# Attention chunk 7 scored and normalized between the last two blocks of the key/value projection

## The chip, the cores and the metric

The kernel runs on one core of one Trainium2 chip, as one launch. Its time is the device time of a whole execution in microseconds (us), median of several. The core's engines run side by side, each with a queue of its own that it works off in order: TensorE (PE, with its weight loads PEld), VectorE (DVE), ScalarE (ACT), GpSimd (POOL) and SyncE (SP), which here issues the transfers (DMA). An instruction that waits holds up all that stands behind it in its engine's queue.

## The reference

One step of a two-layer encoder: layer 0 is an mLSTM mixer with an MLP, layer 1 attention over a band of chunks with an MLP. A prompt of 1024 rows (16 chunks of 64) and a sample of 32 rows with 512 cached rows of keys and values are computed in float32. Layer 1's attention, cut:

```python
kv = (x * (1 + kv_scale) + kv_shift) @ p['w_kv']          # 4 key heads and 4 value heads of 64
q = (u @ p['w_q_b'][lb]).reshape(Bsz, S, NH_B, HD_B)      # 16 query heads, 4 to each key head
def one_chunk(args):                                      # one chunk of 64 queries
    ci, qb = args
    kb = lax.dynamic_slice_in_dim(kp, ci * CHUNK, span, axis=1)   # its own chunk and the 8 before: 576 keys
    vb = lax.dynamic_slice_in_dim(vp, ci * CHUNK, span, axis=1)
    s = jnp.einsum('bqkgd,bskd->bkgqs', qb, kb) * (HD_B ** -0.5) + bias
    s = jnp.where(valid, s, -jnp.inf)
    p = jax.nn.softmax(s, axis=-1)
    return jnp.einsum('bkgqs,bskd->bqkgd', p, vb)
y = o @ p['w_out_b'][lb]
```

A chunk c below 8 has fewer valid keys: (c + 1) * 64, so chunk 7 has 512, and chunks 8 to 15 have 576.

## The kernel before, in words

A matmul operand in float32 is held as two parts, a rounded one (`hi`) and the rest (`lo`); keys are two arrays, `k0` and `k1` (`kk`). SBUF is shared out by tagged rings: `raw` has 3 buffers (inputs and weights as loaded), `wc` 6, the temporary tiles 5. A tile that takes a buffer waits until the last reader of the buffer's former tile is done, and so does a transfer into it.

**The key/value loop** goes over 9 blocks t of rows (8 of 128 prompt rows, one of the 32 sample rows). Block t's input `uk_t` was loaded and split two blocks earlier (`kv_input`); 24 matmuls make the keys, 24 the values (`kv0_t`, `kv1_t`). ACT copies the values to `V`. `put_keys` splits the keys (`kd0` on ACT, `kd1` on DVE), PE transposes them (`kt_n<t>`, and `kt_c<t>` for the cached keys), and four casts on ACT fill `k0` and four on DVE `k1`. The helper `flow` runs pieces of `put_keys` between later blocks' matmuls, so the keys of block 7 are cast after the last block, 8.

**Attention** is a list `todo` of groups (gp, c, e): pair of key heads gp, chunk c (16 is the sample), e one of the pair. A group has two units (query pairs; the sample one). `softmax_unit` makes scores `s` on PE, adds the bias and takes the row extreme in one DVE reduction, and exponentiates on ACT into a tile `p`. `normalize` has a reciprocal on DVE and scales `p` on POOL. `transposed` turns `p` on PE (`pt`), and ACT and DVE copy it in turn to `pT`. `weighted_values` multiplies with `V` (`pv`) and splits the result into `QO`. Names carry the group: `s_0_8_01` is gp 0, chunk 8, e 0, unit 1. PE's queue is in the order in which the program is written: in step n of the loop group n is scored, group n-1 normalized, group n-3 transposed and the pair that ended with n-4 multiplied with `V`. The instructions of the other engines are ordered by the framework's scheduler, which places each by an estimate of when its operands are there, the loads and casts of weights included.

A counter `nun` numbers the units, and its value modulo 12 sets the buffer of `p`: 0 to 4 a temporary tile, 5 to 7 a `raw` tile, 8 to 11 a tile of the attention's own pool. The first blocks of the output weights, `w_ob0_0` and `w_ob0_1` (`wo_block`, `wtile`), are loaded during attention, each in a `raw` buffer (`raw_ob0_0`, `raw_ob0_1`); ACT (L89) and DVE (L90) split them as they split any weight. The issue is written in the list behind the groups (1, 15, e=1) and (1, 9, e=1). Of the output projection (`op_b`), `w_ob0_0` and `w_ob0_1` are the first weights, and `w_ob1_0` the next. The bias table comes in four tiles, `bias0` to `bias3`, loaded after the last block into `wc` buffers.

Of the kernel before, what the change touches and what calls it, by code (L numbers as in the profile page):

```python
# [8 lines left out]
F32 = mybir.dt.float32  # L9
# [6 lines left out]
P = 128  # L16
D = 1024
KC = D // P
TP = 1024
# [56 lines left out]
def trunk_kernel(ctx: ExitStack, tc: tile.TileContext, a, o):  # L76
# [7 lines left out]
    def raw_tile(shape, name):  # L84
        return ring.tile(shape, F32, tag="raw", name=name, bufs=3)
# [99 lines left out]
    def bank(name):  # L185

        bank_n[0] += 1
        return (tpt, nmt, adat, mmt, tpt, nmt, mmt, mmt)[bank_n[0] % 8](name)
# [661 lines left out]
    def tmp_t(shape, name, dt=F32):  # L850
        return T_.tile(shape, dt, tag="t", name=name, bufs=5)
# [847 lines left out]
    def put_keys(src, m, pos, nm):  # L1699

        kd = [tmp_t([P, 256], f"kd{i}_{nm}", F32R) for i in range(2)]
        nc.scalar.copy(kd[0][:m], src)
        nc.vector.tensor_sub(kd[1][:m], src, kd[0][:m].bitcast(F32))
        yield
        ps = bank(f"kt_{nm}").rearrange("p (i b t) -> p i b t", i=2, b=2)
        for i in range(2):
            for b in range(2):
                nc.tensor.transpose(ps[:, i, b, :m], kd[i][:m, b * P:(b + 1) * P].bitcast(F32), ident[:m, :m])
        for i in range(2):
            for g0 in range(2):  # L1710
                for half in range(2):
                    dst = kk[i][64 * half:64 * half + 64, g0::2, pos:pos + m]
                    KCOPY[i][half != g0](dst, ps[64 * g0:64 * g0 + 64, i, :, :m])
# [10 lines left out]
    def kv_input(t):  # L1724
        m = P if t < NT - 1 else TS
        cnd = 0 if t < NT - 1 else 1
        xr = raw_tile([P, KC, P], f"x1_{t}")
        nc.sync.dma_start(xr[:, :, :m], xsp[1][:, :, t * P:t * P + m])
        uk = ring.tile([P, 2, KC, P], F32R, tag="wc", name=f"uk_{t}", bufs=6)
        if m < P:  # L1730
            nc.vector.memset(uk.bitcast(F32), 0.0)
        x = xr[:, :, :m]
        nc.gpsimd.tensor_mul(x, x, kvsc[:, :, cnd:cnd + 1].broadcast_to([P, KC, m]))
        nc.vector.tensor_add(x, x, kvsh[:, :, cnd:cnd + 1].broadcast_to([P, KC, m]))
        split(uk[:, 0, :, :m], uk[:, 1, :, :m], x)
        return uk
# [3 lines left out]
    def cached_keys(t):  # L1740
        cr = tmp_t([P, 256], f"ck_{t}")
        nc.sync.dma_start(cr, ck[t * P:(t + 1) * P])
        nc.sync.dma_start(V[:, 8 + t], cv[t * P:(t + 1) * P])
        yield 3.0
        yield from put_keys(cr, P, TP + t * P, f"c{t}")
    for t in range(NT):
        if t % 2 == 0 and t < 8:
            flow.add(cached_keys(t // 2))
        m = P if t < NT - 1 else TS
        uk = uks[t]  # L1750
        pk = [bank(f"kv{i}_{t}")[:, :256] for i in range(2)]
        for i in range(2):
            for k in range(KC):
                w = wkv[i][k // 4]
                nc.tensor.matmul(pk[i], uk[:, 0, k], w[:, 0, k % 4], start=(k == 0), stop=False)
                nc.tensor.matmul(pk[i], uk[:, 0, k], w[:, 1, k % 4], start=False, stop=False)
                nc.tensor.matmul(pk[i], uk[:, 1, k], w[:, 0, k % 4], start=False, stop=(k == KC - 1))
            if i == 0:
                flow.tick()
        vi = t if t < NT - 1 else 12  # L1760
        nc.scalar.copy(V[:m, vi], pk[1][:m])
        flow.add(put_keys(pk[0][:m], m, t * P if t < NT - 1 else TP + 512, f"n{t}"))
        flow.tick()
        if t >= 4:
            ks = tmp_t([P, 256], f"ks_{t}")
            nc.scalar.copy(ks[:m], pk[0][:m])
            dk, dv = (o["k_p"], o["v_p"]) if t < NT - 1 else (o["k_s"], o["v_s"])
            r0 = (t - 4) * P if t < NT - 1 else 0
            nc.sync.dma_start(dk[0, r0:r0 + m].rearrange("s g d -> s (g d)"), ks[:m])
            nc.sync.dma_start(dv[0, r0:r0 + m].rearrange("s g d -> s (g d)"), V[:m, vi])  # L1770
        if t + 2 < NT:
            uks.append(kv_input(t + 2))
    flow.finish()
    ps0.__exit__(None, None, None)


    at_cm = tc.tile_pool(name="attn", bufs=1, reuse_waits="tile")
    at = at_cm.__enter__()
    psT_cm = tc.tile_pool(name="psT", bufs=1, space=PSUM, reuse_waits="tile")
    psT = psT_cm.__enter__()  # L1780
    bias, sbias = [], []
    for i, (nb, ns) in enumerate(((3, 0), (3, 0), (2, 1), (0, 3))):
        bt = ring.tile([P, 2112], F32, tag="wc", name=f"bias{i}", bufs=6)
        b3 = bt[:, :nb * 576].rearrange("p (b j) -> p b j", j=576) if nb else None
        for hd in range(2 if nb else 0):
            h0 = 2 * len(bias) + hd
            nc.sync.dma_start(b3[64 * hd:64 * hd + 64], bias_d[h0:h0 + 2 * nb - 1:2].rearrange("h i j -> i h j"))
        s3 = bt[:, nb * 576:nb * 576 + ns * 544].rearrange("p (b j) -> p b j", j=544) if ns else None
        for r in range(4 if ns else 0):
            h0 = 4 * len(sbias) + r  # L1790
            nc.sync.dma_start(s3[32 * r:32 * r + 32],
                              bias_d[h0:h0 + 4 * ns - 3:4, :32, :544].rearrange("h i j -> i h j"))
        bias += [b3[:, j] for j in range(nb)]
        sbias += [s3[:, j] for j in range(ns)]

    nun = [0]

    def softmax_unit(qst, g, k0, nk, bt, off, mx, nm):


        s = psT.tile([P, 2, 512], F32, tag="s", name=f"s_{nm}", bufs=2)
        parts = [(0, 0, nk)] if nk <= 512 else [(0, 0, nk // 2), (1, nk // 2, nk // 2)]
        for b, j0, w in parts:
            for i in range(2):
                nc.tensor.matmul(s[:, b, :w], qst, kk[i][:, g, k0 + j0:k0 + j0 + w], start=(i == 0), stop=(i == 1))  # L1805
        nun[0] += 1
        i = nun[0] % 12
        p = tmp_t([P, 640], f"p_{nm}") if i < 5 else raw_tile([P, 640], f"p_{nm}") if i < 8 else \
            at.tile([P, 640], F32, tag="p", name=f"p_{nm}", bufs=4)
        if off:  # L1810
            nc.gpsimd.memset(p[:, :off], 0.0)
        z = p[:, off:off + nk]
        w = parts[0][2]
        np_ = len(parts)
        nc.vector.tensor_tensor_reduce(out=z.rearrange("p (b w) -> p b w", b=np_), in0=s[:, :np_, :w],  # L1815
                                       in1=bt.rearrange("p (b w) -> p b w", b=np_), op0=ALU.add, op1=ALU.min,
                                       scale=-0.125, scalar=3e38, accum_out=mx[:, 0:1])
        nc.scalar.activation(z, z, AF.Exp, bias=mx[:, 0:1], scale=-1.0, accum_out=mx[:, 1:2])
        return p, z
# [50 lines left out]
    class Group:  # L1870
# [15 lines left out]
        def scores(self, pr):  # L1886
            if pr >= self.n:
                return
            bt = bias[2 * self.g + pr][:, 576 - self.nk:] if self.c < 16 else sbias[self.g]
            self.units.append(softmax_unit(qo(self.c)[:, self.e, self.gp, pr * P:(pr + 1) * P], self.g, self.k0, self.nk,  # L1890
                                           bt, self.off, self.mx[:, :, pr], f"{self.nm}_{self.e}{pr}"))

# [25 lines left out]
    for gp in range(2):  # L1918
        for i in range(17):
            c = slim[gp][i // 2] if i % 2 else wide[i // 2] if i < 16 else slim[gp][8]  # L1920
            todo += [(gp, c, e, gp and e and i in (8, 11)) for e in range(2)]
    groups = {}
    with tc.manual_schedule(engines={mybir.EngineType.PE}):
        for n in range(len(todo) + 4):
            new, old, done = n if n < len(todo) else None, groups.get(n - 3), groups.pop(n - 4, None)
            if done and done.e:
                done.values()
            if new is not None:
                groups[n] = Group(*todo[n][:3])
                groups[n].scores(0)  # L1930
            if groups.get(n - 1):
                normalize(groups[n - 1].units, groups[n - 1].mx)
            turn = old.turn() if old else iter(())
            next(turn, None)
            if new is not None:
                groups[n].scores(1)
            for _ in turn:
                pass
            if new is not None and todo[n][3]:
                wo_pre[0, len(wo_pre)] = wo_block(0, len(wo_pre))  # L1940
# [159 lines left out]
```

## Time and profile before

| what | value |
| --- | --- |
| median of 3 runs | 2428.24 us (2427.45 to 2430.74) |
| the profiled execution | 2430.01 us |
| its span in the trace | 2427.9 us |
| PE busy | 97% |
| DVE busy | 81% |
| ACT busy | 49% |
| mean granted PE clock | 0.993 |
| key/value loop ends, attention starts | about 1412 us into the span |
| attention ends, output projection starts | 1616.6 us |

The profiled execution is 1.8 us longer than the median, and 2.1 us of it lie outside the span. Times of places in the trace count from the span's start. PE's busy time includes that at a reduced clock, so a slow stretch does not show as idle: the column of the granted clock shows it.

### The profile page before, as it was taken

The page shows a single profiled execution, that of the slowest core. Times are in us where ns is not written, and L with a number is a line of the kernel's source. Part 1 is how long each engine was busy: PE and PEld are TensorE (multiplying, and loading weights), DVE is VectorE, ACT ScalarE, POOL GpSimd, SP SyncE. Part 2 cuts the span into 40 slices and gives each one's busy share as a digit, 9 for nine tenths or more (in the row PEclk, how much of TensorE's full clock was granted, in tenths as well). Part 3 has the DMA queues.
Part 4 walks back from the last instruction along what each step waited for, and adds up shares of the span by engine and source line. Part 5 has one row for each costly group of instructions (what it writes and reads, how often), then busy time and mean ns, then how long its engine had stood idle before and what let it go on. Part 6 is the DMA issues. An engine that isn't in the chain of part 4 may idle for free.

```text
span 2427.9 us, 44306 instructions
## 1 busy us (share of the span) xinstructions
PE 2361.4 (97%) x17180; PEld 2265.5 (93%) x17180; DVE 1973.8 (81%) x4094; ACT 1180.5 (49%) x2394; POOL 166.5 (7%) x315
## 2 busy tenths in 40 slices
PE   7999999999999999999999999999999999899997
PEld 4999999999999999999989977789999999899997
DVE  4899897778788789989887666756998888887878
ACT  4544456278566630000147466764776777222212
POOL 0111100000000000000001124420000000000003
PEclk9999999999999999999999999999999999999999
DMA  8432322436556896576413220042586779966642
GB/s 295 124 112 87 108 81 90 161 109 206 183 184 203 290 345 244 211 263 216 162 62 100 69 70 1 10 121 57 168 279 222 257 259 337 367 245 235 228 149 72
DMA packets 283702, 423.60 MB, mean 174 GB/s; under 512 B 15320, under 2 KB 205164, under 8 KB 278372
## 3 DMA queue, kind: packets, MB, share of 16 engines
q1 hardware_dynamic: 279460, 390.50, 48.3%
q10 hardware_dynamic: 4032, 30.28, 3.1%
q8 instruction: 135, 2.21, 0.4%
q14 instruction: 75, 0.61, 0.1%
HBM read 304.91 MB, written 118.17 MB: 174 GB/s over the span
## 4 chain that ended last, share of the span: by engine, by line
PE 50%; DVE 10%; DMA 4%; ACT 4%; issue 2%; POOL 1%; SPq 0%; ACTq 0%; DVEq 0%; POOLq 0%
PE dn L1424 11%; PE up L1289 8%; PE dn L120 4%; PE dn L119 4%; PE dn L118 4%; PE pv L1862 3%; PE s L1805 2%; PE pt L1840 2%; DMA radw<-in_w_ada_dram 2%; PE op_b L118 1%; PE op_b L119 1%; DVE wf_u L90 1%; PE op_b L120 1%; DMA rdn_u<-in_w_up_dram 1%; PE up L120 1%
## 5 line engine op out<-in xcount | busy, mean ns | idle before, releaser
L1054 DVE SCALAR_TENSOR_TENSOR ACX<-dn,ada,ACX 128x264 f32<-128x264 f32 (+6 forms) x664 | 281.5, 447 | 84.6 <-PE dn L1424 41.3
L1424 PE MATMUL dn<-fx,wf_d 128*128 128x264 f32 x2016 | 254.0, 285 | 6.4 <-DVE ACX L1054 4.0
L1424 PEld LDWEIGHTS dn<-fx,wf_d 128*128 128x128 f32 x2016 | 248.7, 188 | 8.7 <-DVE ACX L1054 2.7
L89 ACT CAST w_dn<-raw_dn 128x1024 fp32r<-128x1024 f32 x36 | 37.7, 1051 | 284.0 <-DMA raw_dn<-in_w_down_dram 133.1
L118 PE MATMUL dn<-hs,w_dn 128*128 128x384 f32 (+2 forms) x512 | 161.0, 315 | 0.0
L119 PE MATMUL dn<-hs,w_dn 128*128 128x384 f32 (+2 forms) x512 | 160.9, 315 | 0.0
L120 PE MATMUL dn<-hs,w_dn 128*128 128x384 f32 (+2 forms) x512 | 156.4, 314 | 1.3 <-DVE w_dn L90 1.3
L1289 PE MATMUL up<-TF,wf_u 128*128 128x264 f32 x1056 | 143.4, 285 | 3.8 <-ACT H L1292 3.8
L1289 PE MATMUL up<-U,wf_u 128*128 128x264 f32 x1056 | 140.1, 285 | 2.5 <-DVE H L1295 2.0
L1289 PE MATMUL up<-u,wf_u 128*128 128x264 f32 x1056 | 139.7, 285 | 1.6 <-ACT wf_u L89 0.6
L277 DVE SCALAR_TENSOR_TENSOR aw<-radw,cs,aw 128x512 f32<-128x512 f32 x196 | 139.3, 743 | 0.8 <-DMA radw<-in_w_ada_dram 0.8
L1289 PEld LDWEIGHTS up<-TF,wf_u 128*128 128x128 f32 x1056 | 134.2, 188 | 5.1 <-ACT H L1292 5.1
L1289 PEld LDWEIGHTS up<-U,wf_u 128*128 128x128 f32 x1056 | 133.1, 188 | 4.0 <-DVE H L1295 3.0
L1289 PEld LDWEIGHTS up<-u,wf_u 128*128 128x128 f32 x1056 | 132.6, 188 | 2.5 <-ACT wf_u L89 0.8
L119 PE MATMUL dn<-U,w_dn 128*128 128x384 f32 (+2 forms) x416 | 129.8, 313 | 0.0
L118 PE MATMUL dn<-U,w_dn 128*128 128x384 f32 (+2 forms) x416 | 129.4, 312 | 0.3 <-DVE ada L302 0.3
L120 PE MATMUL dn<-U,w_dn 128*128 128x384 f32 (+2 forms) x416 | 125.5, 312 | 0.6 <-DVE w_dn L90 0.6
L120 PEld LDWEIGHTS dn<-hs,w_dn 128*128 128x128 f32 x512 | 95.9, 188 | 2.1 <-DVE w_dn L90 1.7
L119 PEld LDWEIGHTS dn<-hs,w_dn 128*128 128x128 f32 x512 | 96.5, 188 | 0.0
L118 PEld LDWEIGHTS dn<-hs,w_dn 128*128 128x128 f32 x512 | 96.4, 188 | 0.1
L1815 DVE CUSTOM_DVE_ANT_0 p<-s,bias 128x576 f32<-128x576 f32 (+9 forms) x132 | 79.1, 605 | 20.2 <-PE s L1805 13.4
L90 DVE TENSOR_TENSOR HL<-H,HL 128x1056 fp32r<-128x1056 f32 x64 | 80.3, 1254 | 17.5 <-ACT HL L89 17.5
(394 smaller groups left out, 7167.5 us busy)
## 6 DMA issues: line engine op xcount, KB each, us to landing
hpl<-HL SPq DMA_DIRECT2D x144, 264.0 KB
rdn_u<-in_w_up_dram SPq DMA_DIRECT2D x64, 512.0 KB
hd<-HL SPq DMA_DIRECT2D x28, 1056.0 KB
fx<-hd SPq DMA_DIRECT2D x50, 528.0 KB
radw<-in_w_ada_dram SPq DMA_DIRECT2D x24, 1024.0 KB
hd<-HM SPq DMA_DIRECT2D x28, 792.0 KB
raw_up<-in_w_up_dram SPq DMA_DIRECT2D x40, 512.0 KB
raw_dn<-in_w_down_dram SPq DMA_DIRECT2D x36, 512.0 KB
```

The lines of the kernel that those rows point to most:

```text
L90: (eng or nc.vector).tensor_sub(dst_l, src, dst_h.bitcast(F32))
L118: nc.tensor.matmul(ps, wh, mov(0, k), start=(k == 0), stop=False)
L119: nc.tensor.matmul(ps, wh, mov(1, k), start=False, stop=False)
L120: nc.tensor.matmul(ps, wl, mov(0, k), start=False, stop=(k == nk - 1))
L277: nc.vector.scalar_tensor_tensor(acc[cnd], raw[:, k], sc, acc[cnd], op0=ALU.mult, op1=ALU.add)
L1054: nc.vector.scalar_tensor_tensor(xs, ps[:, off + o:off + o + mm_], gate[:, fc, cnd:cnd + 1], xs, op0=ALU.mult, op1=ALU.add)
L1289: nc.tensor.matmul(p, self.ws[w][:, wl, k], moving(f, tp, xl, k), start=first and k + n_ == 0, stop=k == 3 and n_ == 2, skip_group_check=n ...
L1424: nc.tensor.matmul(p, ws[w][:, wl, k], t[:, s0, xl], start=first and k + n_ == 0, stop=k == kg - 1 and n_ == 2, skip_group_check=not first)
L1805: nc.tensor.matmul(s[:, b, :w], qst, kk[i][:, g, k0 + j0:k0 + j0 + w], start=(i == 0), stop=(i == 1))
L1815: nc.vector.tensor_tensor_reduce(out=z.rearrange("p (b w) -> p b w", b=np_), in0=s[:, :np_, :w], in1=bt.rearrange("p (b w) -> p b w", b=np ...
L1840: nc.tensor.transpose(pt[:kp, j - j0, pr * P:(pr + 1) * P], ps_[pr][:, j * P:j * P + kp], ident)
L1862: nc.tensor.matmul(pv[64 * e:64 * e + 64, :nq], V[:kp, vt0 + j, g * 64:(g + 1) * 64], pts[e][:kp, j, :nq], start=(j == 0), stop=(j == nt - 1))
```

## The change

Chunk 7 with the first pair of key heads (groups (0, 7, 0) and (0, 7, 1)) goes to the front of the list. Its scores, reductions, exponentials, and the normalization of e = 0, are placed into the key/value loop: e = 0 ahead of block 7, e = 1 ahead of block 8. The scores take a PSUM bank of the loop's pool. The bias columns that chunk 7 needs are loaded a second time, into two `raw` tiles (`near_0`, `near_1`; 0.5 MB each). The tiles `bias0` to `bias2` are issued after blocks 6, 7 and 8, `bias3` after the loop. The counter `nun` starts at 7, so that chunk 7's four `p` tiles lie in the attention's own pool, and all later units have a number 7 higher than before (chunk 7 of the first pair comes ahead of chunk 8 now). The attention loop starts at step 2 and has the transposes of chunk 7 between the scores of chunk 8. From the scores of the third list entry onward, PE's queue is the former one. The functions `softmax_unit` to `wo_block` are only moved up in the file, ahead of the loop; of them `softmax_unit` and `scores` change in one expression. The diff, cut:

```diff
+    nun, near, groups = [7], {}, {}
-    nun = [0]
...
-        s = psT.tile([P, 2, 512], F32, tag="s", name=f"s_{nm}", bufs=2)
+        s = bank(f"s_{nm}")[:, None] if near else psT.tile([P, 2, 512], F32, tag="s", name=f"s_{nm}", bufs=2)
...
-            bt = bias[2 * self.g + pr][:, 576 - self.nk:] if self.c < 16 else sbias[self.g]
+            bt = near[self.e][:, pr] if near else \
+                bias[2 * self.g + pr][:, 576 - self.nk:] if self.c < 16 else sbias[self.g]
...
     wide, slim = (8, 12, 13, 14, 15, 9, 10, 11), ((7, 6, 5, 4, 16, 3, 2, 1, 0), (16, 7, 6, 5, 4, 3, 2, 1, 0))
             c = slim[gp][i // 2] if i % 2 else wide[i // 2] if i < 16 else slim[gp][8]
+            if not gp and i < 2:
+                c = 7 + i
...
+    def near_bias(e):
+        b = raw_tile([P, 2, 512], f"near_{e}")
+        for hd in range(2):
+            nc.sync.dma_start(b[64 * hd:64 * hd + 64],
+                              bias_d[4 * e + hd:4 * e + hd + 3:2, :, 64:576].rearrange("h i j -> i h j"))
+        return b
+
+    def early(n):
+        groups[n] = Group(*todo[n][:3])
+        for pr in range(2):
+            groups[n].scores(pr)
+        if n:
+            normalize(groups[0].units, groups[0].mx)
+
     for t in range(NT):
         if t % 2 == 0 and t < 8:
             flow.add(cached_keys(t // 2))
+        if t >= NT - 2:
+            early(t - NT + 2)
...
         if t + 2 < NT:
             uks.append(kv_input(t + 2))
+        if t == NT - 3:
+            near.update({e: near_bias(e) for e in range(2)})
+        if t >= NT - 3:
+            bias_load(t - NT + 3)
     flow.finish()
+    near.clear()
     ps0.__exit__(None, None, None)
+    bias_load(3)
...
-        for n in range(len(todo) + 4):
-            new, old, done = n if n < len(todo) else None, groups.get(n - 3), groups.pop(n - 4, None)
-            if done and done.e:
+        for n in range(2, len(todo) + 4):
+            new, done = n if n < len(todo) else None, groups.pop(n - 4, None)
+            old = groups.get(n - 2 if n < 4 else n - 3) if n != 4 else None
+            if done and done.e and n > 5:
                 done.values()
...
+            if n == 4:
+                groups[1].values()
```

`bias_load(i)` has the loads of the former loop over the four bias tiles.

PE's queue at the seam before, from the last transposes of keys (`kt_n8`) to the first transposes of chunk 8:

```order
L1708 MATMUL kt_n8_15634<-ident_64,kd1_n8_15627 128x32 x2
L1805 MATMUL s_0_8_00_15675<-k0_14841,QO1_14267 128x288
...
L1805 MATMUL s_0_8_11_15703<-k1_14842,QO1_14267 128x288
L1805 MATMUL s_0_7_00_15712<-k0_14841,QO1_14267 128x512
...
L1805 MATMUL s_0_7_10_15728<-k1_14842,QO1_14267 128x512
L1840 MATMUL pt_0_8_0_0_15738<-ident_64,p_0_8_00_15680 128x128
```

The same place now:

```order
L1708 MATMUL kt_n8_15685<-ident_64,kd1_n8_15671 128x32 x2
L1775 MATMUL s_0_8_00_15710<-k0_14841,QO1_14267 128x288
...
L1775 MATMUL s_0_8_00_15710<-k1_14842,QO1_14267 128x288
L1810 MATMUL pt_0_7_0_0_15722<-ident_64,p_0_7_00_15489 128x128
...
L1775 MATMUL s_0_8_11_15761<-k1_14842,QO1_14267 128x288
L1810 MATMUL pt_0_7_1_2_15769<-ident_64,p_0_7_10_15581 128x128
```

The scores of chunk 7 have left this place (they stand ahead of blocks 7 and 8), and its transposes stand between the scores of chunk 8.

ACT's queue in the last two blocks now, where before none of the rows at L1788 (exponentials of chunk 7) stood among the casts of keys (L1713) and the splits (L1702):

```order
L1788 ACTIVATE p_0_7_00_15489,mx_0_7_0_15485<-p_0_7_00_15489,mx_0_7_0_15485 128x512
L1713 CAST k0_14841<-kt_n6_15524 64x2x128 x2
L1788 ACTIVATE p_0_7_01_15495,mx_0_7_0_15485<-p_0_7_01_15495,mx_0_7_0_15485 128x512
L1713 CAST k0_14841<-kt_n6_15524 64x2x128 x2
L1702 CAST kd0_n7_15566<-kv0_7_15498 128x256
...
L1788 ACTIVATE p_0_7_10_15581,mx_0_7_1_15577<-p_0_7_10_15581,mx_0_7_1_15577 128x512
L1788 ACTIVATE p_0_7_11_15587,mx_0_7_1_15577<-p_0_7_11_15587,mx_0_7_1_15577 128x512
L1702 CAST kd0_n8_15670<-kv0_8_15593 32x256
L1713 CAST k0_14841<-kt_c3_15619 64x2x128 x4
L1713 CAST k0_14841<-kt_n7_15632 64x2x128 x4
```

All four exponentials now stand ahead of the casts of the last keys (`kt_c3`, `kt_n7`).

ACT's queue around the cast of `w_ob0_0`, near 1568 us, before:

```order
L1849 COPY pT_1_5_0_17528<-pt_1_5_0_0_17529 128x512
L89 CAST w_ob0_0_17551<-raw_ob0_0_17548 128x1024
L1818 ACTIVATE p_1_15_10_17521,mx_1_15_1_17515<-p_1_15_10_17521,mx_1_15_1_17515 128x576
L1818 ACTIVATE p_1_15_11_17540,mx_1_15_1_17515<-p_1_15_11_17540,mx_1_15_1_17515 128x576
L1849 COPY pT_1_5_1_17564<-pt_1_5_1_0_17565 128x512
```

The same place now:

```order
L1788 ACTIVATE p_1_15_10_17527,mx_1_15_1_17521<-p_1_15_10_17527,mx_1_15_1_17521 128x576
L1788 ACTIVATE p_1_15_11_17546,mx_1_15_1_17521<-p_1_15_11_17546,mx_1_15_1_17521 128x576
L1788 ACTIVATE p_1_4_00_17564,mx_1_4_0_17560<-p_1_4_00_17564,mx_1_4_0_17560 128x320
L1788 ACTIVATE p_1_4_01_17580,mx_1_4_0_17560<-p_1_4_01_17580,mx_1_4_0_17560 128x320
L89 CAST w_ob0_0_17557<-raw_ob0_0_17554 128x1024
L1819 COPY pT_1_5_1_17570<-pt_1_5_1_0_17571 128x512
```

The cast has moved behind four exponentials and stands directly ahead of the copy of `pT_1_5_1`, for which `pv_1_5` waits on PE. At `w_ob0_1` ACT's cast likewise moves from ahead of the exponentials of group (1, 10, 0) to behind them, directly ahead of the copy to `pT_1_9_1` on ACT, and on DVE a reduction and the reciprocal of group (1, 10, 0) move ahead of the other copy to `pT_1_9_1`.

More of the change, by code (lines that the diff above doesn't have):

```diff
@@ L1745, in cached_keys, with bias_load @@
         yield from put_keys(cr, P, TP + t * P, f"c{t}")
[L1746 to L1774, printed above, removed]
     at_cm = tc.tile_pool(name="attn", bufs=1, reuse_waits="tile")
     at = at_cm.__enter__()
-    psT_cm = tc.tile_pool(name="psT", bufs=1, space=PSUM, reuse_waits="tile")
-    psT = psT_cm.__enter__()
     bias, sbias = [], []
-    for i, (nb, ns) in enumerate(((3, 0), (3, 0), (2, 1), (0, 3))):
+    def bias_load(i):
+        nb, ns = ((3, 0), (3, 0), (2, 1), (0, 3))[i]
         bt = ring.tile([P, 2112], F32, tag="wc", name=f"bias{i}", bufs=6)
@@ L1792, in trunk_kernel @@
                               bias_d[h0:h0 + 4 * ns - 3:4, :32, :544].rearrange("h i j -> i h j"))
-        bias += [b3[:, j] for j in range(nb)]
-        sbias += [s3[:, j] for j in range(ns)]
-    nun = [0]
+        bias.extend(b3[:, j] for j in range(nb))
+        sbias.extend(s3[:, j] for j in range(ns))
+    nun, near, groups = [7], {}, {}
     def softmax_unit(qst, g, k0, nk, bt, off, mx, nm):
-        s = psT.tile([P, 2, 512], F32, tag="s", name=f"s_{nm}", bufs=2)
+        s = bank(f"s_{nm}")[:, None] if near else psT.tile([P, 2, 512], F32, tag="s", name=f"s_{nm}", bufs=2)
         parts = [(0, 0, nk)] if nk <= 512 else [(0, 0, nk // 2), (1, nk // 2, nk // 2)]
@@ L1920, in trunk_kernel @@
             c = slim[gp][i // 2] if i % 2 else wide[i // 2] if i < 16 else slim[gp][8]
+            if not gp and i < 2:
+                c = 7 + i
             todo += [(gp, c, e, gp and e and i in (8, 11)) for e in range(2)]
-    groups = {}
+    def near_bias(e):
[4 more added lines that the diff above has]
+        return b
@@ new lines, in early @@
+    def early(n):
[4 more added lines that the diff above has]
+            normalize(groups[0].units, groups[0].mx)
+    for t in range(NT):
+        if t % 2 == 0 and t < 8:
+            flow.add(cached_keys(t // 2))
+        if t >= NT - 2:
+            early(t - NT + 2)
+        m = P if t < NT - 1 else TS
+        uk = uks[t]
+        pk = [bank(f"kv{i}_{t}")[:, :256] for i in range(2)]
+        for i in range(2):
+            for k in range(KC):
+                w = wkv[i][k // 4]
+                nc.tensor.matmul(pk[i], uk[:, 0, k], w[:, 0, k % 4], start=(k == 0), stop=False)
+                nc.tensor.matmul(pk[i], uk[:, 0, k], w[:, 1, k % 4], start=False, stop=False)
+                nc.tensor.matmul(pk[i], uk[:, 1, k], w[:, 0, k % 4], start=False, stop=(k == KC - 1))
+            if i == 0:
+                flow.tick()
+        vi = t if t < NT - 1 else 12
+        nc.scalar.copy(V[:m, vi], pk[1][:m])
+        flow.add(put_keys(pk[0][:m], m, t * P if t < NT - 1 else TP + 512, f"n{t}"))
+        flow.tick()
+        if t >= 4:
+            ks = tmp_t([P, 256], f"ks_{t}")
+            nc.scalar.copy(ks[:m], pk[0][:m])
+            dk, dv = (o["k_p"], o["v_p"]) if t < NT - 1 else (o["k_s"], o["v_s"])
+            r0 = (t - 4) * P if t < NT - 1 else 0
+            nc.sync.dma_start(dk[0, r0:r0 + m].rearrange("s g d -> s (g d)"), ks[:m])
+            nc.sync.dma_start(dv[0, r0:r0 + m].rearrange("s g d -> s (g d)"), V[:m, vi])
+        if t + 2 < NT:
+            uks.append(kv_input(t + 2))
+        if t == NT - 3:
+            near.update({e: near_bias(e) for e in range(2)})
+        if t >= NT - 3:
+            bias_load(t - NT + 3)
@@ L1923, in trunk_kernel @@
+    flow.finish()
+    near.clear()
+    ps0.__exit__(None, None, None)
+    bias_load(3)
+    psT_cm = tc.tile_pool(name="psT", bufs=1, space=PSUM, reuse_waits="tile")
+    psT = psT_cm.__enter__()
     with tc.manual_schedule(engines={mybir.EngineType.PE}):
-        for n in range(len(todo) + 4):
-            new, old, done = n if n < len(todo) else None, groups.get(n - 3), groups.pop(n - 4, None)
-            if done and done.e:
+        for n in range(2, len(todo) + 4):
+            new, done = n if n < len(todo) else None, groups.pop(n - 4, None)
+            old = groups.get(n - 2 if n < 4 else n - 3) if n != 4 else None
+            if done and done.e and n > 5:
```

## The prediction

> **What bounds the kernel now.** I read the page's busy shares first, then the windows over the attention stage, then the timelines of TensorE (PE), VectorE (DVE) and ScalarE (ACT) where the change works, and last the timelines around the other places at which the order of the engines' queues changes. The busy shares:
> ```profile
> PE 2361.4 (97%) x17180; PEld 2265.5 (93%) x17180; DVE 1973.8 (81%) x4094; ACT 1180.5 (49%) x2394; POOL 166.5 (7%) x315
> ```
> PE is busy for 97% of the span. A windows row has the stretch, its length, the busy time of PE, of its weight loads, DVE, ACT and POOL, then the granted PE clock, the DMA share and GB/s. Most of attention:
> ```profile
> 1438.00:1560.00 122.00, 120.18 (x904) 96.57 (x904) 84.76 (x276) 85.71 (x235) 52.72 (x98) 1.00 0.01 1
> ```
> Here PE runs at full clock and idles 1.8 us of 122, so whatever makes PE wait in this stage is paid in full, and only stretches with idle PE can be won. The seam between the key/value loop and attention is one. PE's timeline, where the bracket is the idle time ahead of a row and what ended it:
> ```profile
> 1410.45 0.43 PE L1708 MATMUL kt_n<-ident,kd_n 32*128 32x32 f32 x4
> 1412.41 4.67 PE L1805 MATMUL s<-k,QO 128*128 128x288 f32 x18 [1.53 <-DVE k L1713]
> 1417.87 0.74 PE L1805 MATMUL s<-k,QO 128*128 128x512 f32 x2 [0.79 <-DVE mx L1815]
> 1419.40 0.96 PE L1805 MATMUL s<-k,QO 128*128 128x512 f32 x2 [0.79 <-DVE mx L1815]
> 1426.30 0.86 PE L1840 MATMUL pt<-ident,p 128*128 128x128 f32 x4 [2.46 <-POOL p L1826]
> 1434.04 0.65 PE L1805 MATMUL s<-k,QO 128*128 128x448 f32 x2
> 1434.53 0.60 PE L1840 MATMUL pt<-ident,p 128*128 128x128 f32 x4
> 1438.06 0.68 PE L1805 MATMUL s<-k,QO 128*128 128x448 f32 x2
> ```
> The waits are 1.53 + 0.79 + 0.79 + 2.46 = 5.57 us: for the last cast of keys, twice for a reduction that frees a score bank, and for the normalized weights of chunk 8. Behind three of them the clock is halved:
> ```profile
> 1412.80:1416.20 3.40, 3.40 (x15) 3.05 (x14) 2.62 (x7) 1.74 (x4) 0.00 (x0) 0.52 0.89 205
> 1419.90:1423.00 3.10, 3.10 (x15) 2.53 (x13) 1.67 (x8) 2.03 (x7) 1.36 (x2) 0.50 1.08 254
> 1426.60:1429.90 3.30, 3.30 (x18) 2.68 (x17) 1.87 (x4) 0.88 (x2) 0.00 (x0) 0.50 0.00 0
> ```
> Each stretch of about 3.3 us at half clock loses about 1.7 us. The seam thus loses 5.6 + 5.1 = 10.7 us; that is all that the change can win.
>
> **The seam after the change.** PE gets four score units (two 128x512 matmuls each) inside the loop. Rows 1434.04 and 1434.53 show that a pair 448 wide takes 0.49 us until the next row, so a pair 512 wide takes 0.56 and four take 2.2 us; kt_n8 then ends about 1410.6 + 2.2 = 1412.8. These pairs are moved, not added, so only the idle time decides. What they bring along is four reductions on DVE, two reciprocals, and four exponentials on ACT, all placed among the key casts for which the first score s_0_8_00 waits:
> ```profile
> 1403.63 1.73 DVE L1713 CAST k<-kt_n 64x256 fp32r<-64x256 f32 x4 [0.81 <-ACT k L1713]
> 1410.54 2.69 DVE L1713 CAST k<-kt_n 64x256 fp32r<-64x256 f32 x8
> 1417.12 0.69 DVE L1815 CUSTOM_DVE_ANT_0 p<-s,bias 128x512 f32<-128x512 f32 x1 [0.75 <-PE s L1805]
> 1417.73 0.08 DVE L1815 DVE_READ_ACCUMULATOR2_ANT mx<- 128x1 f32 x1
> 1406.87 0.36 ACT L1702 CAST kd_n<-kv 32x256 fp32r<-32x256 f32 x1 [2.55 <-PE kv L1757]
> 1407.26 1.50 ACT L1713 CAST k<-kt_c 64x256 fp32r<-64x256 f32 x4
> 1408.79 1.50 ACT L1713 CAST k<-kt_n 64x256 fp32r<-64x256 f32 x4
> 1417.85 0.72 ACT L1818 ACTIVATE p<-p,mx 128x512 f32<-128x512 f32 x1 [0.60 <-DVE mx L1815]
> 1418.48 0.19 ACT L1818 ACTIVATION_READ_ACCUMULATOR p<-p,mx 128x1 f32 x1
> ```
> A reduction is 0.77 us, an exponential 0.91. ACT had done k0_n6 at 1402.10 + 1.50 = 1403.6 (the DVE row 1403.63 starts then). It now has two exponentials in between: 1405.75, a little over two of them. DVE's k1_n6 follows (1.73: 1407.5), then the split kd1_n7 (1407.9) and two reductions (1409.4). The second exponential of group 1 ends at 1410.4, one behind the last reduction. ACT follows with kd0_n8 (0.36), k0_c3 (1.50), k0_n7 (1.50): 1413.75. DVE casts k1_n7 behind k1_c3 until about 1415.75, and s_0_8_00 starts at 1415.8: 3.0 us idle where there were 1.53. The cover in this stretch is ACT's 2.55 us of idle before 1406.87, which takes nearly three of the four exponentials; without it the delay would be 2.55 more.
>
> From 1415.8 PE does scores and chunk 7's transposes, half clock first, to about 1421.2. Chunk 7's second transposes then wait for a pT copy behind the last exponential of chunk 8: 2.35 us (estimate; the nearest row is the 2.46 removed), and half clock again, 1.7. So the seam has two stalls of 5.35 us and two slow stretches instead of 5.57 us and three. By the chain, s_0_6_10 comes at 1437.1 where 1438.06 stood: **-1.0 us**. If the second wait shrank to the 0.79 of the rows above, -2.5; if the first grew by 1.5, another 1.73 cast in the chain, +0.5.
>
> The two extra tiles of near biases are 1 MB more of loads; each is issued behind a split of an input block, some 8 us ahead of its first reader:
> ```profile
> 1388.95 1.22 DVE L90 TENSOR_TENSOR uk<-x,uk 128x1024 fp32r<-128x1024 f32 x1
> 1394.18 1.23 DVE L90 TENSOR_TENSOR uk<-x,uk 128x1024 fp32r<-128x1024 f32 x1
> ```
> Those splits end at 1390.2 and 1395.4, the first readers come at about 1401.8 and 1407.9. I cost the loads at nothing; after a landing of 4.2 us (below) some 7 us of cover remain. Moved past on SP's queue are only ks and V stores.
>
> **The output weights.** The unit counter that chooses the buffer of each weight tile p starts 7 higher, so raw_ob0_0 and raw_ob0_1 wait for other readers: the transposes pt_1_5_0_2 instead of pt_1_14_0_4, and pt_1_9_0_4 instead of pt_1_4_0_2. The loads' issues before and those new readers:
> ```profile
> 1561.48 1.29 SPq L96 DMA_DIRECT2D raw_ob<-in_w_out_b_dram  x2
> 1580.85 1.25 SPq L96 DMA_DIRECT2D raw_ob<-in_w_out_b_dram  x2
> 1567.76 0.38 PE L1840 MATMUL pt<-ident,p 128*128 128x128 f32 x2
> 1585.51 0.81 PE L1840 MATMUL pt<-ident,p 128*128 128x128 f32 x6
> 1565.00:1566.00 1.00, 1.00 (x10) 0.37 (x6) 0.17 (x1) 0.21 (x2) 0.50 (x1) 1.00 0.31 59
> 1584.00:1585.00 1.00, 1.00 (x8) 0.61 (x9) 0.04 (x1) 0.37 (x1) 0.93 (x3) 1.00 0.52 95
> ```
> The DMA shares 0.31 and 0.52 place the landings at 3.5 to 4.5 us after the issue; I take 4.2. Then raw_ob0_0 is issued at 1568.1 and lands at 1572.3. And what waits for it:
> ```profile
> 1571.05 1.51 PE L1862 MATMUL pv<-pT,V 128*64 128x256 f32 x10 [0.92 <-ACT pT L1849]
> 1567.95 1.05 ACT L89 CAST w_ob<-raw_ob 128x1024 fp32r<-128x1024 f32 x1
> 1570.43 0.57 ACT L1849 COPY pT<-pt 128x512 f32<-128x512 f32 x1
> 1588.42 2.87 PE L1862 MATMUL pv<-pT,V 128*64 128x256 f32 x20
> 1591.22 0.79 PE L1805 MATMUL s<-k,QO 128*128 128x288 f32 x4
> 1571.05:1574.50 3.45, 3.45 (x26) 2.75 (x27) 1.95 (x10) 2.34 (x7) 2.57 (x7) 1.00 0.00 0
> ```
> The cast now stands directly ahead of the copy of pT_1_5_1 on ACT, behind four exponentials: cast 1572.3 to 1573.3, copy, PE goes on at 1573.9 instead of 1571.05: **+2.8**; bounds +1.4 (ACT reaches the cast at 1570.9, data there) and +3.05 (landing 4.5). PE idles 3.75 us. After 0.92 the clock stayed at 1.00 (last row), after 1.53 it halved; so here half clock for 3.4 us: **+1.7** (bounds 0 and 1.7).
>
> At raw_ob0_1 (issue 1586.3, landing about 1590.4) the new order puts a reduction and a reciprocal that waits for an exponential ahead of DVE's copy pT_1_9_1_0: it is done at 1590.4, not 1588.4. The cast ends at 1591.4, ACT's copy of pT_1_9_1_2 behind it lets PE finish from 1592.0. PE idles 1.8 us and runs slow; pv_1_9 ends at about 1595.0 instead of 1591.22: **+3.8**. Bounds: +2.0 (data there, full clock: 1590.4 + 2.87 = 1593.3) and +4.2 (the wait until 1592.0 and then the last 12 of 20 rows, 1.7, at full clock, +2.5, with all of a slow stretch on top). Neither load can gain: both only come later.
>
> A load of two 256 KB pieces here lands in 3.5 to 4.5 us. The Trainium skill, "DMA: Bandwidth & Descriptors" (the two cost components), fits 2.0 us plus bytes over 436 GB/s, an estimate of 3.2 us for 512 KB; by that both landings come 1 us sooner, the first term would be +1.8, the second the same (PE is slow there anyway), and the sum below +6.3. The windows speak against it.
>
> An idle time of 1.53 us sufficed for half clock in this trace. The Trainium skill, "TensorE: Matmul & The Clock Gate" (its cheat-sheet), asks only that no idle gap exceed about 3 us; by that the 1.8 us at raw_ob0_1 would cost no clock, and this term would be +2.5. The trace speaks against it.
>
> The third load of this kind, raw_ob1_0, also comes about 2 us later than its reader did, and its cast goes behind seven ACC scalings:
> ```profile
> 1618.16 1.05 ACT L89 CAST w_ob<-raw_ob 128x1024 fp32r<-128x1024 f32 x1 [1.12 <-DMA raw_ob<-in_w_out_b_dram]
> 1619.76 4.43 ACT L986 ACTIVATE ACC<-ACC,pt 128x288 f32<-128x288 f32 x8 [0.55 <-DMA ACC<-xsp]
> 1640.34 0.31 PE L118 MATMUL op_b<-QO,w_ob 128*128 128x320 f32 x1
> ```
> Its first matmul is that at 1640.34, some 15 us after the cast's new place: nothing.
>
> **The sum.** -1.0 + 2.8 + 1.7 + 3.8 = +7.3 us. The profiled execution took 2430.01 us, 2427.9 of it the span; with the sum 2437.3. It is 1.8 above the median of the runs, 2428.24, so the forecast is 2428.24 + 7.3 = **2435.5 us**. The bounds of the terms add up to +0.9 (-2.5 + 1.4 + 0 + 2.0) and +9.5 (0.5 + 3.05 + 1.7 + 4.2): 2429 to 2438, and with the scatter of the runs (2427.45 to 2430.74) 2439.
>
> **The rivals.** A measurement of this kernel can tell 0.2%, 4.9 us, from no change.
>
> *No difference: the late weights are absorbed.* The loads land by the time ACT reaches the casts and no clock is lost: +1.4 and +2.0, with a seam of -1.0 to -2.5, gives +0.9 to +2.4, about 2430. For it: the issue-to-landing time is known only within 1 us, and the idle limit of the clock only between 0.92 and 1.53. Against it: after 1567.76 a load of 512 KB would have to land within 2.8 us. Chance 0.30, with mixed cases up to +4.9.
>
> *Faster: the seam's stalls all vanish.* If ACT's and DVE's chunk 7 work fits into their idle time in the loop (2.55 us on ACT before 1406.87), PE reaches s_0_8_00 without a wait and the transposes of chunk 7 fill every later one. Then all 10.7 us go; with the least the weights can cost, +3.4, that is -7.3: 2421. The point from which it decides is s_0_6_10 before about 1430. Against it: four exponentials need 3.6 us, and the casts behind them are in the chain to s_0_8_00. Chance 0.10.
>
> *Slower still: the near biases come late.* If a near tile lands after its reduction is due, DVE stands still ahead of the key casts, and PE waits one for one; with a landing 10 us after the issue in place of 4.2, 3 us more and their slow clock: 2440. The margin of 7 us speaks against it. Chance 0.06.
>
> **How the numbers follow.** The forecast's case has 0.54, and with the late biases slower has 0.60; same 0.30, faster 0.10. The range leaves out the faster case (0.10) and about as much at the top: 2427 to 2440.
>
> **What would show it.** Right: PE's first score of attention with about 3.0 us idle, one wait of 2 to 2.5 us about 8 us later, two stretches of clock 0.5 rather than three; s_0_6_10 about 1 us sooner (1437); ACT's casts of w_ob waiting for DMA near 1570 and 1590; PE's pv rows there with 3 to 4 us of idle behind ACT's pT and some 2 us behind DVE's, clock 0.5 behind them. Wrong: issues of raw_ob at 1561 and 1581 as before, a cast's wait under 0.5 us, s_0_6_10 before 1433, or a stall inside the key loop.

## The result and the profile after

The changed kernel takes 2435.53 us (median of 10 runs, 2431.91 to 2441.19), the kernel before 2428.45 (median of 10, 2426.88 to 2433.19): 7.1 us more, a ratio of 1.0027 with a 95% interval of 1.0017 to 1.0036. The forecast was 2435.5 us.

The profiled execution of the changed kernel is one of its longest, 2441.19 us. From its page:

```profile
span 2439.4 us, 44309 instructions
PE 2364.1 (97%) x17180; PEld 2266.3 (93%) x17180; DVE 1977.7 (81%) x4094; ACT 1180.3 (48%) x2394; POOL 163.3 (7%) x315
```

The busy shares tell nothing: PE is busy for 97% of the span, as before. PE's timeline at the seam between the key/value loop and attention, cut to its two waits and the row that the prediction follows:

```profile
1415.83 0.76 PE L1775 MATMUL s<-k,QO 128*128 128x288 f32 x4 [2.56 <-DVE k L1713]
...
1423.45 0.93 PE L1810 MATMUL pt<-ident,p 128*128 128x128 f32 x4 [2.37 <-ACT pT L1819]
...
1435.86 0.67 PE L1775 MATMUL s<-k,QO 128*128 128x448 f32 x2
```

Two waits of 2.56 and 2.37 us stand where there were four with 5.57 us in all, and the last row, `s_0_6_10`, comes 2.2 us sooner than its 1438.06, although the key/value loop began 0.7 us later in this execution (1349.5 against 1348.8). Then the output weights. Before, these were PE's first matmul of `pv_1_5` and the score behind the group:

```profile
1569.49 0.65 PE L1862 MATMUL pv<-pT,V 128*64 128x256 f32 x2
1572.49 0.56 PE L1805 MATMUL s<-k,QO 128*128 128x320 f32 x2
```

The timelines of the changed kernel there follow, PE first (from `pv_1_5`, then from `pv_1_9`), then ACT's two casts, then SP's issues (both loads in one row):

```profile
1567.58 0.65 PE L1832 MATMUL pv<-pT,V 128*64 128x256 f32 x2
1572.80 2.82 PE L1832 MATMUL pv<-pT,V 128*64 128x256 f32 x10 [4.57 <-ACT pT L1819]
1575.55 0.90 PE L1775 MATMUL s<-k,QO 128*128 128x320 f32 x2
...
1592.25 0.65 PE L1832 MATMUL pv<-pT,V 128*64 128x256 f32 x2
1594.22 1.08 PE L1832 MATMUL pv<-pT,V 128*64 128x256 f32 x8 [1.32 <-DVE pT L1821]
1597.31 2.40 PE L1832 MATMUL pv<-pT,V 128*64 128x256 f32 x10 [2.00 <-ACT pT L1819]
1599.64 1.33 PE L1775 MATMUL s<-k,QO 128*128 128x288 f32 x4
...
1571.21 1.04 ACT L89 CAST w_ob<-raw_ob 128x1024 fp32r<-128x1024 f32 x1 [2.39 <-DMA raw_ob<-in_w_out_b_dram]
1595.72 1.04 ACT L89 CAST w_ob<-raw_ob 128x1024 fp32r<-128x1024 f32 x1 [2.35 <-DMA raw_ob<-in_w_out_b_dram]
...
1566.04 26.36 SPq L96 DMA_DIRECT2D raw_ob<-in_w_out_b_dram  x4
```

Both casts wait for their load, both copies of `pT` wait behind the casts, and PE waits for the copies. From the first row of `pv_1_5` to the score behind it PE needs 7.97 us (1567.58 to 1575.55) where it needed 3.00; from the first row of `pv_1_9` to the score behind it 7.39 us where it needed 2.80. The attention stage ended at 1616.56 and ends at 1625.67, the first matmul of the output projection:

```profile
1625.67 0.42 PE L118 MATMUL op_b<-QO,w_ob 128*128 128x320 f32 x1
```

That is +9.1 us in this execution; the other 2.4 us by which its span is longer (2439.4 against 2427.9) lie in the last MLP, whose instructions are the same, and were not traced to a cause. The runs of one kernel scatter by several microseconds, so the terms are taken from the medians of the experiments.

### The profile page after: what moved, and what is told of

Read it like the earlier page. It is cut to its first block, busy times and chain, and to the rows that moved or that the text cites. A ratio compares the mean times of both kernels' runs of the same rounds, so it can differ in the third digit from the quotient of the medians.

```text
span 2439.4 us, 44309 instructions
## 1 busy us (share of the span) xinstructions
PE 2364.1 (97%) x17180; PEld 2266.3 (93%) x17180; DVE 1977.7 (81%) x4094; ACT 1180.3 (48%) x2394; POOL 163.3 (7%) x315
## 5 line engine op out<-in xcount | busy, mean ns | idle before, releaser
L1788 ACT ACTIVATE p<-p,mx 128x576 f32<-128x576 f32 (+9 forms) x132 | 86.5, 656 | 15.9 <-DVE mx L1785 11.7
```

## The experiments

The time of before beside each is the median of the runs made on the same chip. Where two experiments are compared, it is by what each gains or loses against the before beside it. "Former numbers" is the edit of the first experiment.

**1. The former numbers back** (the changed kernel otherwise):

```diff
         for n in range(2, len(todo) + 4):
+            if n in (2, 4):
+                nun[0] = 0 if n == 2 else 8
```

> The changed kernel, but the counter is set to 0 at chunk 8 and to 8 at chunk 12, so that every later unit has its former number and both loads of output weights take the buffers that they took before. Theory (the late weights are the loss, the seam a small gain): 2428.4 - 2.6 = about 2426 us, raw_ob issued near 1559 and 1579, no wait of a cast for DMA. Rival (the loss comes from scoring chunk 7 inside the key loop): it stays at 2435 us. Rival (the phase of the clock's slow stretches makes the difference): between the two, about 2431.

Measured: 2425.52 us (12 runs) beside 2428.38, ratio 0.9984 (0.9975 to 0.9994). The summary of PE's waits between 1560 and 1600 us has one row (us in total, times, longest):

```profile
PE pv L1832 <- ACT pT L1819: 0.9, 1, 0.9
```

That is the 0.92 us of before, and no cast there waits for DMA. The seam alone is a gain of 2.9 us (1.5 to 6.1 by the interval), and renumbering the buffers costs the changed kernel 10.0 (2435.53 against 2425.52).

**2. The counter alone**, on the kernel before: `nun = [7]` for `nun = [0]`.

> The kernel before with one edit: the counter starts at 7. Chunk 7 stays in its old place. Theory (late weights): two waits of a cast for DMA near 1570 and 1590, pv_1_5 and pv_1_9 late by about 5 us each, 2428.4 + 8 to 11 = 2437 to 2439 us, slower than the changed kernel. Rival (scoring in the key loop is the loss): 2428 us.

Measured: 2438.82 us beside 2428.38, ratio 1.0041 (1.0028 to 1.0054): +10.4 us (6.8 to 13.1). The same summary of PE's waits, and ACT's casts:

```profile
PE pv L1862 <- ACT pT L1849: 7.0, 2, 4.7
PE pv L1862 <- DVE pT L1851: 1.3, 1, 1.3
...
1568.06 1.04 ACT L89 CAST w_ob<-raw_ob 128x1024 fp32r<-128x1024 f32 x1 [2.51 <-DMA raw_ob<-in_w_out_b_dram]
1593.15 1.04 ACT L89 CAST w_ob<-raw_ob 128x1024 fp32r<-128x1024 f32 x1 [2.70 <-DMA raw_ob<-in_w_out_b_dram]
```

One number changed, chunk 7 in its old place, and the whole loss is there. The rival that puts the loss on scoring in the key loop falls with these two experiments. The traces agree, one execution each: from the first matmul of the key/value projection to the first of the output projection there are 267.8 us before, 276.2 in the changed kernel, 266.0 in experiment 1 and 279.6 in experiment 2.

**3. Work for PE during the late waits** (changed kernel): ahead of the second matmul of `pv_1_5`, and at the two waits in `pv_1_9`,

```diff
+                for _ in range({("1_5", 0, 1): 14, ("1_9", 0, 1): 4, ("1_9", 2, 1): 6}.get((nm, j, e), 0)):
...
+                    nc.tensor.matmul(fill["t"].rearrange("p a b -> p (a b)"), kk[0][:, 0, 0:P], kk[0][:, 0, 0:512],
+                                     start=True, stop=True)
```

> The changed kernel with 24 added 128x512 matmuls into an unused score tile where PE waits for the late weights: 14 ahead of the second matmul of pv_1_5, 4 and 6 at the two waits in pv_1_9. Nothing reads them; they take some 6 of the 7.9 us of waiting. Theory (part of the loss is half clock after the waits): clock 1.00 behind both places, 3 to 4 us less than the changed kernel, about 2432 us. Rival (the waits alone are the loss, the slow clock is hidden by other waits): 2435 us, or more by the added work.

Measured: 2432.71 us beside 2428.38, ratio 1.0014 (1.0006 to 1.0023). Against the changed kernel's 2435.53 that is -2.8; the two intervals touch, so the size is uncertain, but the clock is not. The windows below have the stretch, its length and PE's busy time first; the granted clock stands ahead of the DMA share. The changed kernel comes first, from `pv_1_5` and from `pv_1_9`, then this one at the same places:

```profile
1567.05:1570.46 3.41, 1.18 (x7) 0.55 (x5) 1.50 (x8) 1.77 (x6) 2.58 (x6) 1.00 0.69 154
1570.46:1573.87 3.41, 1.07 (x6) 0.70 (x8) 1.23 (x1) 1.53 (x2) 0.39 (x3) 0.50 0.00 0
1573.87:1577.29 3.42, 3.42 (x15) 2.23 (x12) 0.92 (x3) 0.37 (x1) 0.00 (x0) 0.50 0.00 0
1594.36:1597.77 3.41, 1.41 (x12) 0.68 (x12) 1.10 (x2) 1.53 (x2) 0.84 (x2) 1.00 0.04 9
1597.77:1601.18 3.41, 3.41 (x14) 2.24 (x11) 0.75 (x3) 0.37 (x1) 0.00 (x0) 0.50 0.00 0
```

```profile
1565.37:1568.79 3.42, 2.35 (x15) 1.25 (x14) 1.23 (x1) 1.75 (x3) 0.23 (x2) 1.00 0.00 0
1568.79:1572.20 3.41, 3.41 (x31) 3.40 (x30) 2.95 (x10) 2.40 (x8) 0.17 (x1) 1.00 0.00 0
1585.85:1589.27 3.42, 2.83 (x15) 1.78 (x16) 1.46 (x3) 1.53 (x2) 1.47 (x2) 1.00 0.11 19
1589.27:1592.68 3.41, 3.41 (x24) 2.29 (x23) 1.11 (x3) 0.37 (x1) 0.00 (x0) 1.00 0.00 0
```

With PE kept at work the clock stays at 1.00 behind both places. By these medians about 3 of the 10 us are slow clock and about 7 the waits themselves.

**4. The last cached keys a block earlier** (former numbers): `flow.add(cached_keys(...))` at t = 0, 2, 4, 5 instead of 0, 2, 4, 6.

> As the first of these kernels (former numbers for all later units), and the last block of cached keys (c3) enters the flow one block earlier, so that only the casts of block 7's keys stand behind chunk 7's exponentials. Theory (the ACT and DVE chain of casts sets the start of attention): the first score starts 0.5 to 2 us sooner after kt_n8, idle 0.6 to 2.1 instead of 2.56, 2423 to 2426 us. Rival (the start is set by PE's own work in the loop or by the bank's release elsewhere): the same idle, 2426 us.

Measured: 2426.40 us beside 2428.38, ratio 0.9993 (0.9984 to 1.0001): no gain over experiment 1. PE's waits ahead of chunk 8's scores:

```profile
1413.72 0.31 PE L1708 MATMUL kt_n<-ident,kd_n 32*128 32x32 f32 x2 [0.55 <-ACT kd_n L1702]
1415.54 0.31 PE L1708 MATMUL kt_n<-ident,kd_n 32*128 32x32 f32 x2 [1.51 <-DVE kd_n L1703]
1417.85 1.30 PE L1775 MATMUL s<-k,QO 128*128 128x288 f32 x4 [0.24 <-DVE k L1713]
```

The expectation was wrong: DVE now had the casts of c3 and n6 ahead of the reductions of e = 1, the exponentials came later, and the same wait came in three pieces, 2.30 us in all. The chain runs through both engines, and moving a link within it freed nothing here.

**5. PSUM banks rotated** (former numbers). Who frees what the first score waits for? Chunk 8 reads no key of block 7, so the wait for the casts of `kt_n7` should be for the PSUM bank that they read, which the score is to write.

```diff
     uks = [kv_input(0), kv_input(1)]
+    for i in range(6):
+        bank(f"pad_{i}")
```

> The first experiment's kernel (former numbers) with six bank allocations ahead of the key loop that nothing uses: they rotate the PSUM banks, so that the first score of attention takes banks that the copy of block 8's values frees, instead of the bank of block 7's transposed keys. Theory (the first wait at the seam is the release of that bank by the last cast of k1, since chunk 8 reads no key of block 7): idle ahead of the first score about 1.1 instead of 2.56, attention about 1.5 us sooner, 2424 us. Rival (the score really waits for keys, or the next step waits as long): the same idle in one piece or in two, 2425.5 us.

Measured: 2422.97 us beside 2427.66, ratio 0.9978 (0.9969 to 0.9987): 1.8 us more gain than experiment 1, though the two intervals overlap. PE's waits at the seam, then DVE's casts of the last keys:

```profile
1410.48 0.80 PE L1777 MATMUL s<-k,QO 128*128 128x288 f32 x4 [1.12 <-ACT V L1931]
1413.59 0.80 PE L1777 MATMUL s<-k,QO 128*128 128x288 f32 x4 [0.91 <-DVE mx L1787]
1417.72 0.66 PE L1812 MATMUL pt<-ident,p 128*128 128x128 f32 x4 [2.37 <-ACT pT L1821]
...
1410.04 2.69 DVE L1713 CAST k<-kt_n 64x256 fp32r<-64x256 f32 x8
```

The first score starts while these casts still run, so it does not read what they write: what it had waited for was the bank. The first wait is 1.12 us, as expected of the copy of the values; 0.91 us come back one step behind, at the reductions. The waits at the seam add up to 4.40 us where experiment 1 has 4.93.

**6. Rotated banks, and work for PE at the second wait** (14 matmuls of 128x256 ahead of the last row above).

> The kernel with rotated banks and 14 added 128x256 matmuls into an unused tile ahead of chunk 7's last transposes, where PE waits 2.37 us. Theory (a stretch of half clock follows a window with too much idle time): no half clock at the seam in any run, 1 to 2 us below the kernel with rotated banks, about 2422.5, and less scatter. Rival (the slow clock only eats other waits): no difference.

Measured: 2421.85 us beside 2427.66, ratio 0.9976 (0.9967 to 0.9985). The wait is 0.71 us and no stretch at the seam is slow in its trace, but the difference to experiment 5, 1.1 us, is within both intervals. It has the lowest median of the study.

```profile
1419.58 0.65 PE L1812 MATMUL pt<-ident,p 128*128 128x128 f32 x4 [0.71 <-ACT pT L1821]
```

**7. Short exponentials** (former numbers): for chunk 7, e = 1, `z[:, :8]` in place of `z` in the activation. The other columns of that chunk stay without their exponential.

> The first experiment's kernel (former numbers), the two exponentials of chunk 7, e = 1, on 8 of 512 columns (the rest of that chunk is left unexponentiated). Theory (ACT's exponentials ahead of the last casts set the start of attention): ACT's casts of c3 and n7 come about 0.9 us sooner, idle ahead of the first score 1.6 to 1.7 instead of 2.56; 1 to 2 us less, about 2424. Rival (the reductions on DVE or PE's extra scores set it): idle stays 2.5, 2425.5 us.

Measured: 2423.16 us beside 2427.66, ratio 0.9982 (0.9974 to 0.9991): 1.6 us more gain than experiment 1 (4.5 against 2.9), within both intervals. An exponential on 8 columns still takes 0.30 us and 0.19 for its sum, and it still waits for its reduction:

```profile
1412.70 0.77 PE L1775 MATMUL s<-k,QO 128*128 128x288 f32 x4 [2.03 <-DVE k L1713]
1406.40 0.30 ACT L1789 ACTIVATE p<-p,mx 128x8 f32<-128x8 f32 x1 [0.24 <-DVE mx L1785]
```

The first wait shrinks by 0.53 us, not by the 0.9 expected: the exponentials are a part of the chain, and the reductions ahead of them are the other.

**8. Work for PE at the four waits of the kernel before** (32 matmuls of 128x256).

> The kernel before with 32 added 128x256 matmuls into an unused tile at its four waits at the seam (8 ahead of the first score, 5 and 5 at the waits for a score bank, 14 ahead of chunk 8's first transposes). Theory (half clock costs what the prediction counted, three times 1.7 us): clock 1.00 throughout the seam, 2428.4 - 3 to 5 = 2423.5 to 2425.5 us. Rival (the waits behind are fixed by ACT, DVE and POOL, so faster matmuls only wait longer): 2427 to 2428 us.

Measured: 2424.98 us beside 2427.66, ratio 0.9992 (0.9983 to 1.0000). No slow stretch is left at its seam. By the medians 2.7 us came of that (0 to 4.1 by the interval), not the 5.1 that the prediction counted; in the two traces the way from `kt_n8` to `s_0_6_10` is 23.79 us instead of 27.61. PE still waits for a reduction there:

```profile
1416.63 0.73 PE L1810 MATMUL s<-k,QO 128*128 128x512 f32 x2 [0.70 <-DVE mx L1820]
```

The rest of the slow clock's price may have been covered by waits for the other engines; this one trace does not settle it.

**9. Rotated banks without the change**: the kernel before, one `bank` allocation ahead of the key loop.

> The kernel before with one bank allocation ahead of the key loop that nothing uses: the first scores of attention take banks that the casts of c3 and the copy ks_8 free. Theory (a bank's release is the whole first wait, 1.53 us): PE starts attention without that wait, but DVE still has 2.7 us of casts ahead of the first reduction, so the wait for a score bank behind it grows: at most 1.5 us and one slow stretch less, 2425 to 2427.5 us, and above the kernel with chunk 7 early and rotated banks (2423). Rival (rotating the banks is all that brought 2423, chunk 7 early nothing): 2423 us.

Measured: 2427.69 us beside 2430.66, ratio 0.9989 (0.9980 to 0.9999). The first wait is gone, and the next one is new:

```profile
1417.17 3.41 PE L1807 MATMUL s<-k,QO 128*128 128x288 f32 x10 [1.95 <-DVE mx L1817]
```

As expected, DVE's casts stand ahead of the first reduction. The waits at this seam add up to 5.99 us, more than the 5.57 before, so the trace, which is of the longest of these runs, does not show where the gain lies. With chunk 7 early and rotated banks the ratio is 0.9978 and the waits are 4.40 us; the intervals still overlap (0.9980 to 0.9987), so that chunk 7's early scoring adds to the rotation is likely and not shown beyond doubt.

## Why the prediction was right, point by point

- **Sign and sum**: +7.3 forecast, +7.1 measured. Both mechanisms were right in the main and both terms too small: the seam -1.0 against -2.9 (experiment 1), the output weights +8.3 (2.8 + 1.7 + 3.8) against +10.0 (the changed kernel against experiment 1) and +10.4 (experiment 2). The errors cancel, so that the forecast came within 0.2 us is luck.
- **The seam's two stalls**: 3.0 and 2.35 us forecast, 2.56 and 2.37 in the trace, and two slow stretches instead of three. The first score came at 1415.83 (1415.8 forecast), but PE ended `kt_n8` at 1413.27, 0.5 us later than worked out; 0.3 of that is a misreading, since the prediction's own row of before ends at 1410.45 + 0.43 = 1410.88 and not at 1410.6. `s_0_6_10` came at 1435.86, not 1437.1: both waits end where the chain put them, but from the end of the second (1423.45) to `s_0_6_10` the trace has 12.4 us, where the forecast times leave 13.5. That last leg is the mis-sized term, and the price of the slow clock is not fixed (below).
- **The chain that sets the first wait** was right as to who ends it, the casts of k1 (ACT's part of the chain ended at 1413.71, forecast 1413.75). It took the score to wait for the keys; experiment 5 shows that it is the release of a PSUM bank. With other banks 1.44 us of the wait went without a faster cast, and 0.91 came back behind it.
- **The late weights**: issue, place in ACT's queue, and the copies behind were right. The mis-sized step is the landing: 4.2 us were taken from where the DMA share falls to nothing, but ACT's cast began 5.2 us after the first issue (1566.04 to 1571.21), although the DMA share was down to 0.01 a microsecond earlier:

```profile
1570.20:1570.40 0.20, 0.00 (x0) 0.00 (x0) 0.00 (x0) 0.00 (x0) 0.20 (x1) 1.00 0.01 0
```

  So PE waited 4.57 us, not 3.75, and 1.32 + 2.00 at `pv_1_9`, not 1.8. The end of a transfer's traffic is not the time at which its reader may go.
- **The slow clock behind these waits** is there, and longer than one stretch behind the first (two, 6.8 us, of which the first is mostly waiting). Experiment 3 puts the slow clock of both places at about 3 us together.
- **The rivals**: "absorbed" and "near biases late" did not come. DVE did not wait for the near tiles; by the prediction's own times they were issued some 12 us ahead of their readers, not the 8 that it states. The faster rival did not come either: its sign was `s_0_6_10` before about 1430, and stalls of 4.93 us remain at the seam. The seam does gain, and with the weights undone the kernel is faster than before (experiment 1).
- **The DMA page** (the Trainium skill, "DMA: Bandwidth & Descriptors", the two cost components) made the landing 3.2 us by an estimate; the trace has 5.2, further off than the 4.2 taken here. The page gives that fit for transfers issued by GpSimd; these are issued by SP. The same page's breakdown of the fixed cost says that the semaphore follows only when the last byte is confirmed; that agrees with the 1.0 us between 1570.2 and ACT's start at 1571.21.

## What to carry to other kernels

A counter that deals out buffers is part of the schedule: shifting it by a few moves loads that are written hundreds of instructions later, because the load waits for whoever last read the buffer. Look up for each such load which reader it now waits for, what stands behind its cast, and who waits for that. And where a first instruction of a stage waits for something that it doesn't read, ask which buffer or bank it is given.

## What the runs showed of the hardware

The slow stretches lie on a fixed grid. In the changed kernel's trace they begin at 1416.86, 1423.69, 1570.46 and 1597.77, all multiples of 3.413 us apart (2, 43 and 8 of them), and each lasts 3.41 us, the one at 1570.46 twice that. What counts is how much of a wait falls into one window of this grid. The changed kernel's windows at the seam come first, then those of experiment 3, which has the same two waits there (2.55 and 2.37 us):

```profile
1413.45:1416.86 3.41, 1.03 (x9) 1.06 (x9) 3.24 (x11) 1.61 (x7) 0.00 (x0) 1.00 0.78 155
1416.86:1420.28 3.42, 3.42 (x18) 3.39 (x17) 1.75 (x5) 1.74 (x4) 0.00 (x0) 0.50 0.99 243
1420.28:1423.69 3.41, 1.04 (x8) 0.81 (x8) 1.96 (x7) 2.62 (x6) 2.01 (x3) 1.00 1.08 233
1423.69:1427.10 3.41, 3.41 (x18) 2.38 (x18) 1.46 (x3) 1.06 (x3) 0.92 (x2) 0.50 0.10 18
```

```profile
1411.77:1415.18 3.41, 1.83 (x15) 1.86 (x16) 3.11 (x11) 1.01 (x6) 0.00 (x0) 1.00 0.73 172
1415.18:1418.59 3.41, 1.83 (x16) 1.59 (x13) 2.40 (x7) 3.16 (x8) 1.40 (x2) 1.00 1.04 246
1418.59:1422.01 3.42, 2.63 (x22) 2.02 (x24) 2.12 (x5) 1.69 (x5) 1.53 (x3) 1.00 0.86 179
```

The kernel before had its first wait in one window:

```profile
1409.49:1412.90 3.41, 1.88 (x17) 1.67 (x16) 3.27 (x10) 2.21 (x9) 0.00 (x0) 1.00 0.43 70
1412.90:1416.32 3.42, 3.42 (x15) 2.95 (x13) 2.64 (x9) 1.74 (x4) 0.00 (x0) 0.50 0.92 211
```

In the changed kernel 2.4 us of idle time in one window halve the next. In experiment 3 the edges fall elsewhere, the same waits leave 1.6 us in each of two windows, and the clock stays whole. Yet the 1.53 us of before, in one window, did halve the next, so near this value idle time alone does not decide. Over the eleven traces, without their first 15 and last 25 us, each window at full clock with 1.9 us of idle time or more was followed by one at half clock, none with less than 1.1 was, and between the two both occur.

The seam shows what this is worth. The changed kernel, experiment 1 and experiment 3 have the same work for PE there and the same two waits. Their rows of `kt_n8`, and of `s_0_6_10` in the two experiments (the changed kernel's, at 1435.86, is shown above):

```profile
1412.84 0.43 PE L1708 MATMUL kt_n<-ident,kd_n 32*128 32x32 f32 x4
...
1411.75 0.43 PE L1708 MATMUL kt_n<-ident,kd_n 32*128 32x32 f32 x4
1436.09 0.68 PE L1775 MATMUL s<-k,QO 128*128 128x448 f32 x2
...
1410.37 0.43 PE L1708 MATMUL kt_n<-ident,kd_n 32*128 32x32 f32 x4
1430.19 0.67 PE L1775 MATMUL s<-k,QO 128*128 128x448 f32 x2
```

From the one to the other PE takes 23.02 us in the changed kernel's trace, with two slow stretches, 24.34 in experiment 1's, with three, and 19.82 in experiment 3's, with none. So up to 4.5 us at this seam hang on how the grid lies in an execution, and a fixed number of slow stretches, as the prediction counts them, is not a property of the kernel. The grid's place against the span's start differs from trace to trace; that this is the scatter of the runs of one kernel is likely and was not tried.

The Trainium skill, "TensorE: Matmul & The Clock Gate" (Part 1), speaks of a free-running window of about 3.4 us; the traces agree. The limit of about 3 us for an idle gap in the same page's table "Why this matters for your kernels", which the prediction calls its cheat-sheet, is too long here: gaps of 2.56 and 2.37 us were followed by half clock.
